# One transformer layer on one core: pairs of column tiles, the top-k search and its masks, and the copies of the normed input rearranged

## The chip, the cores and the metric

The kernel runs on one core of a Trainium2 chip. The metric is the device time of one execution in microseconds (us). A change of over 0.2% (5 us here) is about what a measurement of this kernel can tell from no change.

The core's engines work side by side and wait for each other through semaphores: TensorE (PE, matrix products, results in the accumulator memory PSUM), VectorE (DVE), ScalarE (ACT), GpSimd (POOL) and SyncE (SP, which here only starts DMA transfers). Each engine takes its own instructions strictly in the order in which the program lists them.

## The reference, cut to what matters

```python
h = rmsnorm(x, pre_norm_mix) * (1 + scale_m) + shift_m          # (1024, 1024)
proj = h @ w_in                                                # q_lat, kv_lat, k_idx, w_idx, z, xbc, dt, g_a, g_b
# A: sparse attention: a score for every pair of positions, the best 256 keys of each query
iscore = sum_h w_idx * relu(q_idx[h] @ k_idx.T)                # -inf for later chunks
idx = top_k(iscore, 256)
y_a = softmax(q @ kv[idx] * scale + bias) @ kv[idx] @ w_uv @ w_o_attn
# B: Mamba-2 mixer: causal convolution of width 4 over xbc, SiLU, chunked scan, gate silu(z)
y_b = ssd(silu(conv(xbc)), z, dt) @ w_o_ssd
x = x + gate_m * rmsnorm((sigmoid(g_a)*y_a + sigmoid(g_b)*y_b) @ w_out)
x = x + gate_f * rmsnorm((silu(h2 @ wg) * (h2 @ wu)) @ w_ffn_out)
```

All of it is in float32. A float32 product is made of three products of split operands: each operand is kept as a rounded part (`hi`) and a rest (`lo`), and hi·hi, hi·lo and lo·hi are added up in PSUM. So every weight tile passes through ACT (`hi`, a copy that rounds) and POOL (`lo`, raw minus hi) before PE can use it.

## The kernel before, in words

The input h is held as eight tiles of 128 features by 1024 positions, each in two halves of 512 positions (`Hs[k][hi or lo][half]`). The stages that matter here follow one another in the program, and a scheduler, which has a model of the engines, interleaves them. The program's order is its priority.

1. **The input** (`k_h`, L364). x is normed and scaled into h. Each half tile of h in full precision is also written to DRAM (`d_h`), from ACT's queue (L375, L438).
2. **First projections, convolution tiles, indexer.** PE multiplies h by columns of `w_in`. `conv` (L776) is one convolved tile: 48 products of 128x512 in two PSUM banks, one ACT copy for each, nine DVE operations that add the shifted taps (L783 to L785), then SiLU. `convs(FIRST)` (L896) makes five groups of four tiles. Beside them the indexer (L599 to L637) adds 16 heads into the scores `acc[i]`, one SBUF tile for each block i = 2 to 7 of 128 queries, (i+1)·128 keys wide.
3. **Sums for pairs** (L640 to L658). Copies of h come back from `d_h` and are combined on DVE into the operands of a seven-product scheme (Winograd's form of Strassen's) for two column tiles and two halves of positions; `d_h12` saves those parts of h whose places are used up.
4. **Pairs of column tiles** (`h_early`, `h_pair`, L847 to L899). For the twelve pairs that make z and the gate g_a, two products of 12 matmuls each were made early (`h_early`); `h_pair` makes the other five. It loads four weight halves (a11, a12, a21, a22), adds them up (`hs` s1 on DVE, L864; s2 and others on POOL, L865, L879, L883), turns each into hi and lo (L820 ACT, L821 POOL), and DVE reads the products out of PSUM in five additions (L873 twice, L881, L885, L893). Three PSUM banks serve these products. a22's place (tag `vt`, L856) exists once.
5. **The search** (`Ranked`, L663 to L733). The 256 best keys of a query are found by a search for the 256th score, bit by bit, for all six blocks at once: 33 steps. In a step, a candidate value for each block (`cand`, one column of 128 values for each) is compared with all scores. ACT counts for blocks 7, 5 and 2 (L692), DVE for 6, 4 and 3 (L680, an operation that also sums what it writes, followed by a read of the sum). Then four DVE operations on 128x6 values decide and make the next candidate: `tm` = count <= bound (L685), `tm` = tm·cand (L686), `c` = max(c, tm) (L687), `cand` from `c` and `ce` (L727, in the first eight steps L721). All of these small tiles are in SBUF.
6. **The masks** (`mark`, L735). Six passes over each block's scores turn the found value into a mask of 0 and -1e30 (`MK[i]`), ties taken in order (L738 to L747). They are made for all blocks together, straight after the search.
7. **Attention** (L1035), eight head pairs of four query groups each, in the order u = 0, 2, 1, 3. u = 0 needs no mask; u = 2 needs blocks 4 and 5. The first operation that adds a mask or bias to scores is L962. The last three convolution groups (`convs(LATER)`, L1080) and further products fill PE beside it.

The weight stream `W` has three hi and three lo places and loads two tiles ahead of the one in use.

Of the kernel before, what the change touches and what calls it, by code (L numbers as in the profile page):

```python
# [67 lines left out]
def build(tc, a, dbg=None, stop=99, slots=None):  # L68
# [290 lines left out]
        ada_end(k, acc)  # L359
        first[k] = split(Q, raw, "p1", (P, 3, P), lo_eng=G)  # L360

    raws = []

    def k_h(k, b):  # L364
        x = X0[k][b]
        V.tensor_tensor(x, x, rx[b], op=OP.mult)
        hi, lo = H_(f"h{k}h", dt=F32R), H_(f"h{k}l", dt=F32R)
        i1 = S.activation(hi, x, AF.Identity, bias=mod[:, k:k + 1], scale=amul[:, k:k + 1])
        V.tensor_scalar(x, x, amul[:, k:k + 1], mod[:, k:k + 1], op0=OP.mult, op1=OP.add)
        i2 = (G if b else V).tensor_tensor(lo, x, f(hi), op=OP.subtract)  # L370
        if k == 5:
            barrier.update((i.ins.engine, i.ins.name) for i in (i1, i2))
        Hs[k][0][b], Hs[k][1][b] = hi, lo
        for t, dst in raws:
            S.dma_start(dst, t)  # L375
        raws[:] = [(x, d_h[k][:, half(b)])]
        dump("h", x, (k, slice(None), half(b)))

    def k_mm(k, b):
# [17 lines left out]
    with in_order(*ORDERED):  # L397
        sums = [None, None], [None, None]
        x_squares(0, range(8), sums[0])
        r0 = rstd(sums[0], D)  # L400
        k_ada(0)
        pr0 = rspread(r0)
        k_mod(0)
        rx[0] = Q("rx")
        S.activation(rx[0], pr0, AF.Copy)
        pp1 = [[(bank if t or b else bank_d)(f"pp{t}") for b in BS] for t in range(3)]
        k_h(0, 0)
        k_ada(1)
# [12 lines left out]
        k_mod(2)  # L421
        k_h(0, 1)
        k_h(1, 1)
        k_mm(0, 1)
        k_mm(1, 1)
        for k in range(AHEAD, KT):
            k_h(k, 0)
            k_h(k, 1)
            if k < KT - 1:
                i = k_load(k + 1).ins  # L430
                barrier[i.engine] = i.name
                k_ada(k + 1)
            k_mm(k, 0)
            if k < KT - 1:
                k_mod(k + 1)
            k_mm(k, 1)
        for t, dst in raws:
            S.dma_start(dst, t)  # L438
        const_loads()
        nA = con.tile([P, 32], F32, name="nA")  # L440
        S.activation(nA, alb, AF.Exp)
# [197 lines left out]

    XH = {n: [None] * 4 for n in ("11", "21", "22", "1", "2", "3", "4")}  # L640
    for j in range(4):
        for i in range(2):
            SP.dma_start(d_h12[j, i], f(Hs[j][i][1]))
    for j in range(4):
        top, low = R("htop"), R("hlow")
        SP.dma_start(top, d_h[j])
        SP.dma_start(low, d_h[4 + j])
        b11, b12, b21, b22 = (t[:, half(b)] for t in (top, low) for b in BS)
        for n, k, b in (("11", j, 0), ("21", 4 + j, 0), ("22", 4 + j, 1)):
            XH[n][j] = Hs[k][0][b], Hs[k][1][b]  # L650
        V.tensor_tensor(b11, b12, b11, op=OP.subtract)
        XH["1"][j] = split(Q, b11, "ht", lo_eng=G)
        V.tensor_tensor(b12, b22, b12, op=OP.subtract)
# [9 lines left out]
    class Ranked:  # L663
# [3 lines left out]
        def __init__(self, on_s, on_v):  # L667
            self.tiles, self.ns = on_s + on_v, len(on_s)
            self.n = [(i + 1) * P for i in self.tiles]
            for name in ("c", "ce", "cand", "cnt", "kk", "ks", "kv", "sg", "tm"):  # L670
                setattr(self, name, sm.tile([P, len(self.tiles)], F32, name=name + "_", tag="rk" + name, bufs=1))
            self.junk = [Q("junk", (P, 1024), BF) for _ in range(2)]

        def rows(self):
# [6 lines left out]

        def take(self, sl, bound):

            c, cand, tm = self.c[:, sl], self.cand[:, sl], self.tm[:, sl]
            V.tensor_tensor(tm, self.cnt[:, sl], bound[:, sl], op=OP.is_le)  # L685
            V.tensor_tensor(tm, tm, cand, op=OP.mult)  # L686
            V.tensor_tensor(c, c, tm, op=OP.max)  # L687
# [29 lines left out]
        def bits(self):  # L717
# [9 lines left out]
                V.scalar_tensor_tensor(cand, self.ce, 2.0 ** -e, c, op0=OP.mult, op1=OP.add)  # L727
                self.step()
            sl = slice(0, self.ns)
            V.scalar_tensor_tensor(cand[:, sl], c[:, sl], 1.5 * 2.0 ** -24, c[:, sl], op0=OP.mult, op1=OP.add)  # L730
            V.tensor_scalar(cand[:, sl], cand[:, sl], TINY, None, op0=OP.max)
            self.count_v(OP.is_lt, cand, self.rows()[sl])
            self.take(sl, self.kv)  # L733

        def mark(self):  # L735

            for x, y in self.rows():
                V.tensor_scalar(y, y, self.c[:, x:x + 1], self.sg[:, x:x + 1], op0=OP.subtract, op1=OP.mult)  # L738
            self.count_v(OP.is_gt, 0.0, self.rows())
            V.tensor_scalar(self.tm, self.cnt, -1.0, float(TOPK), op0=OP.mult, op1=OP.add)  # L740
            for x, d in self.rows():
                eq, run = R("eq")[:, 0:self.n[x]], R("run")[:, 0:self.n[x]]
                V.tensor_scalar(eq, d, 0.0, None, op0=OP.is_equal)
                V.tensor_tensor_scan(run, eq, eq, 0.0, op0=OP.add, op1=OP.max)
                V.scalar_tensor_tensor(run, run, self.tm[:, x:x + 1], eq, op0=OP.is_le, op1=OP.mult)
# [9 lines left out]
    best = Ranked((7, 5, 2), (6, 4, 3))  # L755
    best.start()
    best.bits()
    best.mark()
    if dbg is not None and "mk" in dbg:
        for i in MK:  # L760
            n = (i + 1) * P
# [28 lines left out]
            S.activation(t, t, AF.Silu)  # L790
            SP.dma_start(dst, t)

    def conv_group(g, n):

        tiles = ((16 + g, d_bc[g, 0]), (24 + g, d_bc[g, 1]), (2 * g, d_xs[2 * g]), (2 * g + 1, d_xs[2 * g + 1]))
        for i in range(0, 4, n):
            outs = [o for t in tiles[i:i + n] for o in conv(*t)]
            if n > 1:
                with in_order(mybir.EngineType.Activation):
                    conv_out(outs[::-1])  # L800
# [2 lines left out]

    n_x = iter(range(GROUPS))

    def convs(kinds):
        for kind in kinds:
            conv_group(next(n_x), 2 if kind == "X" else 1)


    PAIRS = [((1 + t, d_z[t]), (2 + t, d_z[t + 1]), AF.Silu) for t in range(0, 16, 2)]
# [40 lines left out]
    def h_pair(n):  # L852
        (ca, da), (cb, db), fn = PAIRS[n]
        a11, a12 = (hw(W.tile(0, F32), ca, h) for h in range(2))
        a21 = hw(wp.tile([P, 4, P], F32, name="a21", tag="adaw", bufs=2), cb, 0)
        a22 = hw(vp.tile([P, 4, P], F32, name="a22", tag="vt", bufs=1), cb, 1)  # L856
        if n < H_EARLY:
            p, p1 = bank_d("ph"), EV("p1")
            SP.dma_start(p1, d_q1[n])
# [797 lines left out]
```

## Time and profile before

| | |
|---|---|
| median of 3 runs | 2538.54 us (2537.05 to 2541.62) |
| the profiled execution | 2529.57 us |
| its span, first to last instruction | 2527.3 us |
| PE busy in the span | 2388.9 us (95%), 11802 matmuls |
| DVE, ACT, POOL busy | 1591.7 (63%), 1211.8 (48%), 1139.5 us (45%) |
| DMA | 372.72 MB, mean 147 GB/s |

A profile row of a group gives the program line, the engine, the operation, output<-inputs by the program's tile names, shapes and count; behind the bar the busy time in us and the mean of one in ns; behind the second bar the engine's idle time before them and what ended it. A row of the timeline gives the start, the duration, and in brackets the idle time before it. Rows by stretch of time give the busy time of each engine with its number of instructions, then the TensorE clock that was granted (1.00 is full), the share of the DMA engines and GB/s.

### The profile page before, as it was taken

How to read it: one execution, taken by the hardware profiler on the slowest of the kernel's cores; microseconds unless marked ns; L12 is line 12 of the kernel's file. 1: busy time of each engine (PE TensorE's matmuls, PEld its weight loads, DVE VectorE, ACT ScalarE, POOL GpSimd, SP SyncE). 2: the span in 40 equal slices, each digit the busy share in tenths (PEclk: the TensorE clock that was granted, in tenths of full speed). 3: DMA queues.
4: the chain of work that ended last, by engine and by line, in shares of the span. 5: the costliest groups of instructions: out<-in, count | busy, mean ns of one | idle time of the engine just before them, and what ended most of it. 6: DMA issues, size and time to landing. Idle time of an engine off the chain costs nothing. (4 is left out here: it accounts for less than half of the span.)

```text
span 2527.3 us, 35118 instructions
## 1 busy us (share of the span) xinstructions
PE 2388.9 (95%) x11802; PEld 1919.3 (76%) x11802; DVE 1591.7 (63%) x2984; ACT 1211.8 (48%) x2331; POOL 1139.5 (45%) x909
## 2 busy tenths in 40 slices
PE   6999999988868999999999999999999999999996
PEld 5788888766557887777776776888777888888886
DVE  3465767899997556767557767346476666543336
ACT  3445666566624454555666556454445222343111
POOL 2432213645554344555234444656667554532233
PEclk8999999989989999999999999999999999999998
DMA  8234242533353222222578676565375444344132
GB/s 311 104 105 143 81 137 101 196 113 108 117 171 103 85 99 92 89 88 79 179 221 259 217 236 220 186 212 192 125 246 167 163 156 152 117 150 147 46 101 88
DMA packets 228675, 372.72 MB, mean 147 GB/s; under 512 B 23008, under 2 KB 87184, under 8 KB 228496
## 3 DMA queue, kind: packets, MB, share of 16 engines
q1 hardware_dynamic: 225472, 365.72, 43.9%
q10 hardware_dynamic: 3024, 4.77, 0.5%
q8 instruction: 93, 1.52, 0.3%
q14 instruction: 86, 0.70, 0.1%
HBM read 273.65 MB, written 99.90 MB: 148 GB/s over the span
## 5 line engine op out<-in xcount | busy, mean ns | idle before, releaser
L152 POOL TENSOR_TENSOR wlo<-wraw,whi 128x512 fp32r<-128x512 f32 (+1 forms) x234 | 319.7, 1367 | 564.2 <-ACT whi L151 493.5
L151 ACT ACTIVATE whi<-wraw 128x512 fp32r<-128x512 f32 (+1 forms) x234 | 145.5, 623 | 319.4 <-PE pfo L231 111.4
L1419 PE MATMUL p<-xh,wr 128*128 128x512 f32 x880 | 274.2, 391 | 2.7 <-DVE g L1469 2.7
L1413 POOL TENSOR_TENSOR wr<-a,wr 128x512 fp32r<-128x512 f32 x110 | 154.4, 1417 | 101.8 <-ACT wr L1412 68.4
L1419 PEld LDWEIGHTS p<-xh,wr 128*128 128x128 f32 x880 | 166.0, 189 | 37.7 <-DVE g L1469 3.2
L1419 PE MATMUL p<-xl,wr 128*128 128x512 f32 x440 | 171.9, 391 | 0.0
L965 ACT ACTIVATE lg<-lg,mx 128x256 f32<-128x256 f32 (+7 forms) x128 | 98.3, 769 | 96.2 <-DVE mx L962 93.4
L322 POOL TENSOR_TENSOR adaw<-adaw,cs 128x512 f32<-128x512 f32 x64 | 69.6, 1087 | 128.5 <-DMA adaw<-ada_w 119.6
L1412 ACT ACTIVATE wr<-a 128x512 fp32r<-128x512 f32 x110 | 67.7, 628 | 122.8 <-PE p L1419 95.7
L231 PE MATMUL pfo<-ah,wlo 128*128 128x512 f32 x304 | 118.1, 389 | 0.0
L231 PE MATMUL pfo<-al,whi 128*128 128x512 f32 x304 | 117.9, 389 | 0.0
L231 PE MATMUL pfo<-ah,whi 128*128 128x512 f32 x304 | 117.8, 389 | 0.0
L637 DVE SCALAR_TENSOR_TENSOR acc<-rel,widx,acc 128x384 f32<-128x384 f32 (+2 forms) x90 | 92.1, 1046 | 37.5 <-ACT rel L632 37.3
L1534 DVE TENSOR_TENSOR facc<-facc,pfo 128x512 f32<-128x512 f32 x64 | 44.0, 687 | 112.0 <-PE pfo L231 112.0
L1419 PE MATMUL p<-h2h,wr 128*128 128x512 f32 x352 | 112.3, 396 | 0.0
L692 ACT ACTIVATE junk<-acc,cand__2341 128x1024 bf16<-128x1024 f32 (+2 forms) x96 | 86.2, 898 | 54.3 <-DVE cand__2341 L727 38.0
L828 PE MATMUL ph<-hth,whi 128*128 128x512 f32 x192 | 83.5, 435 | 23.2 <-DVE g L873 12.0
L231 PE MATMUL pos<-yw,whi 128*128 128x512 f32 x256 | 101.3, 396 | 3.8 <-DVE yw L1262 3.6
L231 PE MATMUL pos<-yh,whi 128*128 128x512 f32 x256 | 100.6, 393 | 1.7 <-ACT yh L1261 1.7
L231 PE MATMUL pos<-yh,wlo 128*128 128x512 f32 x256 | 99.9, 391 | 0.0
L828 PE MATMUL ph<-hth,wlo 128*128 128x512 f32 x192 | 81.7, 436 | 18.2 <-POOL wlo L821 18.1
L1419 PEld LDWEIGHTS p<-xl,wr 128*128 128x128 f32 x440 | 82.9, 188 | 17.3
(642 smaller groups left out, 7220.6 us busy)
## 6 DMA issues: line engine op xcount, KB each, us to landing
wraw<-w_in SPq DMA_DIRECT2D x130, 256.0 KB, 2.7
a<-w_ffn_in SPq DMA_DIRECT2D x124, 256.0 KB, 3.1
adaw<-ada_w SPq DMA_DIRECT2D x64, 256.0 KB, 2.6
al<-d_ac SPq DMA_DIRECT2D x32, 512.0 KB, 5.5
wraw<-w_o_ssd SPq DMA_DIRECT2D x64, 256.0 KB, 3.2
al<-d_a SPq DMA_DIRECT2D x44, 256.0 KB, 5.1
d_a<-g SPq DMA_DIRECT2D x40, 256.0 KB, 2.5
ada<-ada_p SPq DMA_DIRECT2D x16, 512.0 KB, 5.9
```

The lines of the kernel that those rows point to most:

```text
L151: behind(S.activation(hi[:, :kt], raw[:, :kt], AF.Copy))
L152: behind(G.tensor_tensor(lo[:, :kt], raw[:, :kt], f(hi[:, :kt]), op=OP.subtract))
L231: T.matmul(o, wt[:, k0 + i, :], xs[k][xi][b][:, sl], start=pi == 0 and i == 0 and wt is hi and xi == 0, stop=pi == len(pcs) - 1 and i == l ...
L322: behind(G.tensor_tensor(t, t, cs[:, 4 * h:4 * h + 4, None].to_broadcast([P, 4, P]), op=OP.mult))
L637: V.scalar_tensor_tensor(acc[i][:, 0:n], rel[:, 0:n], ws, acc[i][:, 0:n], op0=OP.mult, op1=OP.add)
L692: S.activation(self.junk[0][:, 0:self.n[x]], y, AF.Sign, scale=-1.0, bias=self.cand[:, x:x + 1], accum_out=self.cnt[:, x:x + 1])
L828: T.matmul(p, w[wi][:, i], XH[x][i][xi], start=start and i == 0 and k == 0, stop=i == 3 and k == 2, skip_group_check=True)
L965: S.activation(lg[:, 0:n], lg[:, 0:n], AF.Exp, scale=-1.0, bias=m, accum_out=mx[:, 3:4])
L1412: S.activation(w[:, 0], src, AF.Copy)
L1413: G.tensor_tensor(w[:, 1], src, f(w[:, 0]), op=OP.subtract)
L1419: T.matmul(p, w[:, wi, i], X[x][i][xi], start=start and i == 0 and k == 0, stop=i == 3 and k == 2, skip_group_check=True)
L1534: V.tensor_tensor(fv, fv, p[b], op=OP.add)
```

## The change

Five edits, with the line numbers of the kernel before:

- `h_pair`: a22 lies in `vt` for odd pairs and in another existing place (`ul`, which the weights of the indexer and of attention use) for even ones.
- `Ranked`: `c`, `ks`, `kv` and `tm` become columns of one PSUM bank, taken from the five that other stages share. `tm·cand` gets a place of its own in SBUF, `got`. So each of a step's four small operations has an input in PSUM and at most one in SBUF. Two copies are added at the search's end: c to `got`, and c to `found` in SBUF, from which the masks are made.
- `mark` makes one block's mask. It is called in the order 4, 5, 2, 3, 6, 7, and it stands behind the pairs in the program, with the first of the three later convolution groups: two calls inside that group, four behind it. The other two groups stay where they were.
- The writes of h to `d_h` from ACT's queue go. In their place, behind the start of the indexer, POOL adds hi and lo of each half into a tile `hraw` (one place, 128x1024) and SP writes it, eight times.
- The writes to `d_h12` move behind those.

```diff
 def k_h(k, b):
...
-        for t, dst in raws:
-            S.dma_start(dst, t)
-        raws[:] = [(x, d_h[k][:, half(b)])]
...
+    with tc.issue_after(next(i for i in reversed(nc.cur_bb.bb.instructions) if i.engine == mybir.EngineType.Pool)):
+        for k in range(KT):
+            t = vp.tile([P, L], F32, name="hraw", tag="vt", bufs=1)
+            for b in BS:
+                G.tensor_tensor(t[:, half(b)], f(Hs[k][0][b]), f(Hs[k][1][b]), op=OP.add)
+            ins = SP.dma_start(d_h[k], t).ins
+    with tc.issue_after(ins):
+        for j in range(4):
+            for i in range(2):
+                SP.dma_start(d_h12[j, i], f(Hs[j][i][1]))
...
-            for name in ("c", "ce", "cand", "cnt", "kk", "ks", "kv", "sg", "tm"):
+            for name in ("found", "cand", "cnt", "kk", "sg", "ce", "got"):
                 setattr(self, name, sm.tile([P, len(self.tiles)], F32, name=name + "_", tag="rk" + name, bufs=1))
+            rk = bank("rank")
+            for i, name in enumerate(("c", "ks", "kv", "tm")):
+                setattr(self, name, rk[:, 8 * i:8 * i + len(self.tiles)])
...
             V.tensor_tensor(tm, self.cnt[:, sl], bound[:, sl], op=OP.is_le)
-            V.tensor_tensor(tm, tm, cand, op=OP.mult)
-            V.tensor_tensor(c, c, tm, op=OP.max)
+            V.tensor_tensor(got, tm, self.cand[:, sl], op=OP.mult)
+            V.tensor_tensor(c, c, got, op=OP.max)
...
-        def mark(self):
+        def mark(self, i):
...
-    best.mark()
...
-        a22 = hw(vp.tile([P, 4, P], F32, name="a22", tag="vt", bufs=1), cb, 1)
+        a22 = hw((vp if n % 2 else wp).tile([P, 4, P], F32, name="a22", tag="vt" if n % 2 else "ul", bufs=1), cb, 1)
...
+    marks = iter((4, 5, 2, 3, 6, 7))
+    convs(LATER[0], lambda: best.mark(next(marks)))
+    for i in marks:
+        best.mark(i)
...
-    convs(LATER)
+    convs(LATER[1:])
```

What the scheduler makes of it, at three places. The first is DVE in the middle of the search, beside a pair in the middle of the twelve. `g` and `u` are products read out of PSUM, `junk,cnt` are counts, the rest the small operations. Before:

```order
L685 TENSOR_TENSOR tm__2347<-cnt__2342,ks__2344 128x6
L686 TENSOR_TENSOR tm__2347<-tm__2347,cand__2341 128x6
L687 TENSOR_TENSOR c__2339<-c__2339,tm__2347 128x6
L873 TENSOR_TENSOR g_5698<-ph,p_5676 128x512
L727 SCALAR_TENSOR_TENSOR cand__2341<-ce__2340,c__2339 128x6
L680 TENSOR_SCALAR junk,cnt__2342<-acc_997,cand__2341 128x896
L680 TENSOR_SCALAR junk,cnt__2342<-acc_995,cand__2341 128x640
L873 TENSOR_TENSOR u_5699<-ph,p_5676 128x512
L680 TENSOR_SCALAR junk,cnt__2342<-acc_999,cand__2341 128x512
```

The same place in the changed kernel, whose lines are numbered a little higher and where `rank` is the PSUM bank:

```order
L689 TENSOR_TENSOR rank<-cnt__2357,rank 128x6
L878 TENSOR_TENSOR g_5879<-ph,p_5857 128x512
L690 TENSOR_TENSOR got__2361<-rank,cand__2356 128x6
L691 TENSOR_TENSOR rank<-rank,got__2361 128x6
L731 SCALAR_TENSOR_TENSOR cand__2356<-ce__2360,rank 128x6
L684 TENSOR_SCALAR junk,cnt__2357<-acc_981,cand__2356 128x896
L684 TENSOR_SCALAR junk,cnt__2357<-acc_979,cand__2356 128x640
L878 TENSOR_TENSOR u_5880<-ph,p_5857 128x512
L684 TENSOR_SCALAR junk,cnt__2357<-acc_1023,cand__2356 128x512
```

The kinds of operation are the same; each small one now names `rank`. Counted over DVE's whole list, 33 steps stand ahead of the last product of the twelfth pair (L893) before, and 27 in the changed kernel: six steps moved behind the pairs.

The second place is DVE straight behind the search's 32nd step before (the last pair's products are still to come; `acc` rows are the first pass of the masks):

```order
L730 SCALAR_TENSOR_TENSOR cand__2341<-c__2339 128x3
L738 TENSOR_SCALAR acc_997<-acc_997,c__2339,sg__2346 128x896
L738 TENSOR_SCALAR acc_995<-acc_995,c__2339,sg__2346 128x640
L738 TENSOR_SCALAR acc_999<-acc_999,c__2339,sg__2346 128x512
L731 TENSOR_SCALAR cand__2341<-cand__2341 128x3
L873 TENSOR_TENSOR g_6133<-ph,p_6111 128x512
```

and in the changed kernel a step behind the last pair, with the taps of a convolved tile (`cv`) between:

```order
L684 TENSOR_SCALAR junk,cnt__2357<-acc_981,cand__2356 128x896
L787 SCALAR_TENSOR_TENSOR cv<-pw,vec,cv 128x511
L684 TENSOR_SCALAR junk,cnt__2357<-acc_979,cand__2356 128x640
L324 TENSOR_REDUCE adas<-adaw 128x128
L684 TENSOR_SCALAR junk,cnt__2357<-acc_1023,cand__2356 128x512
L788 SCALAR_TENSOR_TENSOR cv<-pw,vec,cv 128x1
L789 SCALAR_TENSOR_TENSOR cv<-pw,vec,cv 128x511
L787 SCALAR_TENSOR_TENSOR cv<-pw,vec,cv 128x510
L689 TENSOR_TENSOR rank<-cnt__2357,rank 128x6
```

The end of the search and the masks now lie among convolved tiles. Counted up to the first L962, DVE has six sets of tap rows (L783) behind the pairs before and fifteen now; PE has 113 convolution matmuls (`pw`) between the last pair product and the first score product of attention before, and 249 now.

The third place is POOL at the start of the indexer (`wlo` are the lo parts of weight tiles, `r` a small power). Before:

```order
L152 TENSOR_TENSOR wlo<-wraw,whi 128x512 x2
L270 TENSOR_TENSOR r<-v,nhalf 128x4
L152 TENSOR_TENSOR wlo<-wraw,whi 128x512 x11
L270 TENSOR_TENSOR r<-v,nhalf 128x4
L152 TENSOR_TENSOR wlo<-wraw,whi 128x512
```

and now:

```order
L270 TENSOR_TENSOR r<-v,nhalf 128x4
L567 TENSOR_TENSOR hraw<-h0h,h0l 128x512 x2
L152 TENSOR_TENSOR wlo<-wraw,whi 128x512 x2
L567 TENSOR_TENSOR hraw<-h1h,h1l 128x512 x2
L567 TENSOR_TENSOR hraw<-h2h,h2l 128x512 x2
L152 TENSOR_TENSOR wlo<-wraw,whi 128x512
L567 TENSOR_TENSOR hraw<-h3h,h3l 128x512 x2
L152 TENSOR_TENSOR wlo<-wraw,whi 128x512
L567 TENSOR_TENSOR hraw<-h4h,h4l 128x512 x2
L152 TENSOR_TENSOR wlo<-wraw,whi 128x512
```

Sixteen additions now stand among the weight parts, two for each tile of h. On SP's queue the eight writes of `hraw` stand one by one between loads of weights (L150), and the eight writes to `d_h12`, which were among the first loads of the program, stand behind the last of them.

More of the change, by code (lines that the diff above doesn't have):

```diff
@@ L360, in k_mod @@
         first[k] = split(Q, raw, "p1", (P, 3, P), lo_eng=G)
-    raws = []
     def k_h(k, b):
@@ L436, in build @@
             k_mm(k, 1)
-        for t, dst in raws:
-            S.dma_start(dst, t)
         const_loads()
@@ L641, in build @@
     for j in range(4):
-        for i in range(2):
-            SP.dma_start(d_h12[j, i], f(Hs[j][i][1]))
-    for j in range(4):
         top, low = R("htop"), R("hlow")
@@ L682, in take @@
         def take(self, sl, bound):
-            c, cand, tm = self.c[:, sl], self.cand[:, sl], self.tm[:, sl]
+            c, tm, got = self.c[:, sl], self.tm[:, sl], self.got[:, sl]
             V.tensor_tensor(tm, self.cnt[:, sl], bound[:, sl], op=OP.is_le)
-            V.tensor_tensor(tm, tm, cand, op=OP.mult)
-            V.tensor_tensor(c, c, tm, op=OP.max)
+            V.tensor_tensor(got, tm, self.cand[:, sl], op=OP.mult)
+            V.tensor_tensor(c, c, got, op=OP.max)
         def step(self):
@@ L729, in bits @@
             sl = slice(0, self.ns)
-            V.scalar_tensor_tensor(cand[:, sl], c[:, sl], 1.5 * 2.0 ** -24, c[:, sl], op0=OP.mult, op1=OP.add)
+            V.tensor_copy(self.got[:, sl], c[:, sl])
+            V.scalar_tensor_tensor(cand[:, sl], self.got[:, sl], 1.5 * 2.0 ** -24, c[:, sl], op0=OP.mult, op1=OP.add)
             V.tensor_scalar(cand[:, sl], cand[:, sl], TINY, None, op0=OP.max)
@@ L733, in bits @@
             self.take(sl, self.kv)
-        def mark(self):
[L737 to L741, printed above, removed]
+            V.tensor_copy(self.found, c)
+        def mark(self, i):
+            for x, d in [self.rows()[self.tiles.index(i)]]:
+                V.tensor_scalar(d, d, self.found[:, x:x + 1], self.sg[:, x:x + 1], op0=OP.subtract, op1=OP.mult)
+                self.count_v(OP.is_gt, 0.0, [(x, d)])
+                V.tensor_scalar(self.kk[:, x:x + 1], self.cnt[:, x:x + 1], -1.0, float(TOPK), op0=OP.mult, op1=OP.add)
                 eq, run = R("eq")[:, 0:self.n[x]], R("run")[:, 0:self.n[x]]
@@ L744, in mark @@
                 V.tensor_tensor_scan(run, eq, eq, 0.0, op0=OP.add, op1=OP.max)
-                V.scalar_tensor_tensor(run, run, self.tm[:, x:x + 1], eq, op0=OP.is_le, op1=OP.mult)
+                V.scalar_tensor_tensor(run, run, self.kk[:, x:x + 1], eq, op0=OP.is_le, op1=OP.mult)
                 V.scalar_tensor_tensor(run, d, 0.0, run, op0=OP.is_gt, op1=OP.max)
@@ L791, in conv_out, with conv_group @@
             SP.dma_start(dst, t)
-    def conv_group(g, n):
+    def conv_group(g, n, beside):
         tiles = ((16 + g, d_bc[g, 0]), (24 + g, d_bc[g, 1]), (2 * g, d_xs[2 * g]), (2 * g + 1, d_xs[2 * g + 1]))
@@ L797, in conv_group @@
             outs = [o for t in tiles[i:i + n] for o in conv(*t)]
+            beside()
             if n > 1:
@@ L804, in build, with convs @@
     n_x = iter(range(GROUPS))
-    def convs(kinds):
+    def convs(kinds, beside=lambda: None):
         for kind in kinds:
-            conv_group(next(n_x), 2 if kind == "X" else 1)
+            conv_group(next(n_x), 2 if kind == "X" else 1, beside)
     PAIRS = [((1 + t, d_z[t]), (2 + t, d_z[t + 1]), AF.Silu) for t in range(0, 16, 2)]
```

## The prediction

> **What bounds the kernel now.** I first read the busy time by stretches of time, cut at the stages of the program.
>
> ```profile
> 318.00:442.00 124.00, 124.00 (x578) 104.04 (x577) 80.81 (x113) 81.30 (x159) 28.58 (x20) 1.00 0.37 119
> 442.00:518.00 76.00, 67.94 (x279) 52.89 (x279) 62.94 (x98) 41.20 (x76) 48.90 (x33) 0.96 0.55 181
> 518.00:708.00 190.00, 156.56 (x605) 116.69 (x603) 177.23 (x368) 127.82 (x253) 102.11 (x82) 0.95 0.33 113
> 708.00:782.00 74.00, 51.64 (x213) 41.80 (x214) 71.84 (x100) 12.35 (x21) 39.97 (x27) 0.84 0.49 164
> 782.00:960.00 178.00, 178.00 (x1024) 146.73 (x1023) 105.39 (x331) 94.10 (x178) 69.41 (x66) 1.00 0.28 94
> ```
>
> The first pair of numbers behind the stretch is PE's busy time and count, then weight loads, DVE, ACT, POOL. Ahead of 442 us and behind 782 us PE is busy without a gap. Between 518 us (the first pair's last sum) and 782 us (attention's first L962) it isn't, and there DVE is busy for 177.23 + 71.84 = 249.1 of 264 us, 94%. The pairs, the search and the masks run in this stretch: DVE bounds it, PE the stages on both sides.
>
> How much PE loses follows from the pace of matmuls that wait for nothing: the first and the last of twelve in a row.
>
> ```profile
> 722.73 0.39 PE L828 MATMUL ph<-h4h,whi 128*128 128x512 f32 x1
> ...
> 725.22 0.39 PE L828 MATMUL ph<-h7h,wlo 128*128 128x512 f32 x1
> ```
>
> They start (725.22 - 722.73) / 11 = 0.226 us apart. The 605 of the second stretch need 137 us and take 190. So a pair of 60 matmuls needs 13.6 us and takes 18.8.
>
> PE's waits in 518 to 782 us, with total, number and longest, and the longest one's row:
>
> ```profile
> PE ph L828 <- POOL wlo L821: 17.7, 10, 1.8
> PE pw L231 <- DVE cv L784: 17.1, 2, 14.8
> PE ph L828 <- DVE g L873: 12.0, 7, 3.2
> ...
> 760.90 1.19 PE L231 MATMUL pw<-h,whi 128*128 128x512 f32 x2 [14.77 <-DVE cv L784]
> ```
>
> Two of the three end on DVE; the long one falls among the masks, where PE has run ahead into the later convolutions, its three PSUM banks are full, and DVE's taps stand behind mask passes. The first wait is a chain that begins on DVE: `hs`, POOL, ACT, POOL.
>
> What fills DVE, as groups from 440 to 825 us (mean ns is the number ahead of the second bar):
>
> ```profile
> L680 DVE TENSOR_SCALAR_CACHE_REDUCE junk<-acc,cand__2341 128x896 bf16<-128x896 f32 (+4 forms) x99 | 91.3, 922 | 2.2
> L727 DVE SCALAR_TENSOR_TENSOR cand__2341<-ce__2340,c__2339 128x6 f32<-128x6 f32 x23 | 17.1, 744 | 0.6
> L687 DVE TENSOR_TENSOR c__2339<-c__2339,tm__2347 128x6 f32<-128x6 f32 (+1 forms) x33 | 15.6, 473 | 0.8
> L686 DVE TENSOR_TENSOR tm__2347<-tm__2347,cand__2341 128x6 f32<-128x6 f32 (+1 forms) x33 | 14.9, 451 | 1.1 <-DVE tm__2347 L685 0.2
> L685 DVE TENSOR_TENSOR tm__2347<-cnt__2342,ks__2344 128x6 f32<-128x6 f32 x32 | 10.3, 322 | 5.3 <-ACT junk L692 3.7 <-DVE junk L680 0.5
> L783 DVE SCALAR_TENSOR_TENSOR cv<-pw,vec,cv 128x511 f32<-128x511 f32 (+2 forms) x13 | 9.6, 736 | 1.5 <-ACT cv L780 1.5
> L873 DVE TENSOR_TENSOR u<-ph,p 128x512 f32<-128x512 f32 x12 | 8.2, 685 | 0.0
> L653 DVE TENSOR_TENSOR htop<-hlow,htop 128x512 f32<-128x512 f32 x4 | 4.9, 1235 | 2.5 <-DMA hlow<-d_h 2.5
> L721 DVE TENSOR_SCALAR cand__2341<-c__2339 128x6 f32<-128x6 f32 x8 | 4.7, 582 | 0.2
> L784 DVE SCALAR_TENSOR_TENSOR cv<-pw,vec,cv 128x1 f32<-128x1 f32 (+2 forms) x12 | 2.5, 209 | 1.6 <-ACT cv L780 1.6
> ```
>
> 129 operations on six columns (L727, L687, L686, L685, L721) take 62.6 us. The timeline says why. DVE at the end of two steps, and POOL beside it:
>
> ```profile
> 706.22 1.21 DVE L686 TENSOR_TENSOR tm__2347<-tm__2347,cand__2341 128x6 f32<-128x6 f32 x1
> ...
> 707.95 0.70 DVE L687 TENSOR_TENSOR c__2339<-c__2339,tm__2347 128x6 f32<-128x6 f32 x1
> 708.69 1.20 DVE L727 SCALAR_TENSOR_TENSOR cand__2341<-ce__2340,c__2339 128x6 f32<-128x6 f32 x1
> ...
> 713.25 0.17 DVE L686 TENSOR_TENSOR tm__2347<-tm__2347,cand__2341 128x6 f32<-128x6 f32 x1
> 713.46 0.17 DVE L687 TENSOR_TENSOR c__2339<-c__2339,tm__2347 128x6 f32<-128x6 f32 x1
> ```
>
> ```profile
> 706.12 1.28 POOL L883 TENSOR_TENSOR wraw<-wraw,hs 128x512 f32<-128x512 f32 x1
> 707.37 2.50 POOL L821 TENSOR_TENSOR wlo<-hs,whi 128x512 fp32r<-128x512 f32 x2
> ```
>
> The same operation takes 1.21 us while POOL works and 0.17 us while it doesn't, and the slow ones end with POOL's: 707.43 against 707.40, 709.89 against 709.87. They are locked out by POOL. L873, whose inputs are one in PSUM and one in SBUF, is not: 0.685 us on average, in the same company, while L653, of the same size with both inputs in SBUF, takes 1.235.
>
> **The change part by part.** Times are the profiled execution's: a span of 2527.3 us in 2529.6. The median of the runs is 2538.5, 9 us above it; I carry the difference over.
>
> *Small operations in PSUM.* Each has now one SBUF input at most, like L873. Their price without POOL: the trace has no 128x6 operation on PSUM; the nearest is L784 (a PSUM input, one column) at 0.209, and dependent ones add about 0.04 (0.21 between the starts of L686 and L687 at 0.17 each). I take 0.25: 129 x 0.25 = 32 us instead of 62.6, 30 us saved. Bounds: 0.17, the clean SBUF row, saves 41; 0.40, near L686's mean today, saves 11. [...]
>
> *Masks and steps beside convolutions.* DVE does six of its 33 steps and all masks behind the pairs, among 15 sets of taps instead of 6. Up to the first L962 that adds 9 L783, 8 L785 of the same length and 8 L784: 17 x 0.736 + 8 x 0.209 = 14 us. The masks' passes are the same; the two copies cost 0.4.
> DVE's work in the stretch is then 249 - 30 + 14 = 233 us. What share of the time will it be busy? In a pair it has five sums and `hs` (6 x 0.685 = 4.1), and 27/11 = 2.45 steps of three counts (3 x 0.922) and four small ones (1.0): 9.2. That is 13.3 us against PE's 13.6: equal, so neither hides the other's delays as DVE does today at 94%. I take 91%: 233 / 0.91 = 256, and L962 starts at 518 + 256 = 774, 8 us earlier. At 94% it is 17 us, at 88% it is 1 us later. What is late next is PE itself in the pairs and still DVE behind them.
> By then PE has done 249 - 113 = 136 more matmuls of the later convolutions: 136 x 0.226 = 31 us that the stage behind, which PE bounds (178 of 178 us), no longer has to do. Together 39 us.
>
> *a22's second place.* It lets the loads of the next pair run earlier, against the 17.7 us of waits for `wlo`. As DVE bounds the stretch I count nothing; the cover is DVE's 13.3 us in a pair. If DVE had more room it would be worth up to those 17.7.
>
> *Less to fill attention with.* Without filler attention runs like this:
>
> ```profile
> 1000.00:1200.00 200.00, 194.69 (x1389) 151.62 (x1388) 140.84 (x540) 106.68 (x246) 116.60 (x119) 1.00 0.26 85
> ```
>
> 97%, against 100% with it: up to 5 us over the 178; I take 2 lost.
>
> *Copies of h.* The writes from ACT's queue fell in part into the first 63 us, where the DMA engines carry 311 GB/s:
>
> ```profile
> GB/s 311 104 105 143 81 137 101 196 113 108 117 171 103 85 99 92 89 88 79 179 221 259 217 236 220 186 212 192 125 246 167 163 156 152 117 150 147 46 101 88
> d_h<-x ACTq DMA_DIRECT2D x16, 256.0 KB, 2.2
> ```
>
> If half of the 16 and of the eight `d_h12` writes fall there, 3.1 MB go: at most 10 us; I take 2, since other waits remain. The additions cost POOL 16 x 1.3 us where it is mostly idle, but each of the eight rounds holds POOL until SP's 512 KB write lands, with weight parts behind it, and SP's loads of weights behind the write. Their pace and the price of a landing:
>
> ```profile
> 172.40 1.29 POOL L152 TENSOR_TENSOR wlo<-wraw,whi 128x512 fp32r<-128x512 f32 x1 [8.53 <-ACT whi L151]
> 175.12 1.30 POOL L152 TENSOR_TENSOR wlo<-wraw,whi 128x512 fp32r<-128x512 f32 x1 [1.43 <-ACT whi L151]
> 184.48 1.29 POOL L152 TENSOR_TENSOR wlo<-wraw,whi 128x512 fp32r<-128x512 f32 x1 [8.06 <-ACT whi L151]
> ...
> vt<-d_v SPq DMA_DIRECT2D x8, 512.0 KB, 3.6
> ada<-ada_p SPq DMA_DIRECT2D x16, 512.0 KB, 5.9
> ```
>
> Two parts are wanted every 12.1 us, one every 6.0. A round takes 2.6 + 3.6 to 2.6 + 5.9 = 6.2 to 8.5 us and lets one part through. Seven rounds fall 1 to 18 us behind; loading two tiles ahead covers 12.1. So 0 to 5 us; I take 2 lost.
>
> Sum: 39 - 2 + 2 - 2 = 37 us. 2529.6 - 37 = 2492.6 for a profiled execution, 2538.5 - 37 = 2501 for the median. With one bound at a time it is 2489 (0.17 us), 2522 (0.40 us), 2493 (94%) and 2510 (88%); 0.17 us with all 10 us of the writes gives 2481. So this case reaches from 2481 to 2522.
>
> **The rivals.**
> *The copies bound the first stage (slower).* A round's write stands on SP behind writes that wait for ACT, or lands late, and PE, which has no gap there, waits for `wlo`. A round of c us costs 7 x (c - 6.0) - 12.1. It eats the 39 us and 5 more from c = 14.0; at 15 it costs 51 and the time is 2550. For it: the single place of `hraw` and the strict queues. Against: 256 KB writes land in 2.2 us. Chance 0.07.
> *The lock stays.* If an output in SBUF is enough to be locked out, the small operations keep their 62.6 us: 249 + 14 = 263, at 94% 279 us, L962 15 us later, 31 - 15 - 2 = 14 us gained: 2524. Against it stands L873, which writes to SBUF. Chance 0.12. [...]
> *The credit is lost.* If attention needs that filler, only the 8 us are left: 2530. Against: the 97%. Chance 0.08.
> *Both engines full.* At 0.17 and 94%, 222 us of work take 236: 28 + 31 us, less nothing else: 2479. Chance 0.12.
> *It comes to nothing.* Small losses of each kind add up to the gain, within 5 us of 2538.5. Chance 0.06.
>
> **How the numbers follow.** The forecast has 0.55. 0.2% (5 us) is about what a measurement tells from no change. Faster: 0.55 + 0.12 + 0.12 + 0.07 of the lost credit = 0.86; the same 0.07; slower 0.07. The range from 2474 to 2531 holds most of the forecast, of the full engines, of the staying lock and half of the lost credit, about 0.8.
>
> **What would show it.** In the changed profile the small operations' means should lie near 0.25 us whatever POOL does; a mean over 0.4 is the staying lock. The first L962 should start near 774 us, and a pair should take about 15 us of PE instead of 18.8. The 14.77 us wait should be gone. Ahead of 442 us PE should stay without gaps; gaps behind `wlo` near 160 to 220 us are the slower rival. If the stretch to L962 isn't shorter and the stage behind it not shorter by some 30 us, the argument is wrong.

## The result, and the profile after

The changed kernel takes 2471.34 us (median of 4, 2468.4 to 2477.29), the kernel before on the same chip 2537.8 us: a ratio of 0.9743, with an interval of 0.9717 to 0.9769. The forecast was 2501 us with a range from 2474 to 2531, so the direction was right and the gain, 66 us, was nearly double the 37 forecast. Between the two profiled executions the spans differ by 60.7 us; the profile accounts below add up to that.

The busy time by stretches of the changed kernel, cut where the prediction cut the old one: two stretches ahead of the first pair's last sum (513.1 us), the eleven further pairs up to the twelfth's last sum (660.7 us), the time behind them up to the first addition of a mask or bias (749.0 us; it was 782.2), and the attention behind. The prediction had 774 us for this addition. The columns are those of the prediction's first fence.

```profile
311.00:436.00 125.00, 125.00 (x582) 104.87 (x582) 81.14 (x114) 81.83 (x159) 28.06 (x20) 1.00 0.38 119
436.00:513.10 77.10, 69.06 (x298) 53.90 (x297) 65.50 (x87) 42.18 (x78) 54.01 (x35) 1.00 0.56 187
513.10:660.70 147.60, 146.77 (x647) 120.97 (x646) 130.79 (x351) 119.05 (x235) 109.39 (x87) 1.00 0.54 174
660.70:749.00 88.30, 69.23 (x297) 55.92 (x296) 83.50 (x163) 33.21 (x60) 36.27 (x28) 0.92 0.39 128
749.00:926.00 177.00, 169.52 (x1016) 138.50 (x1016) 106.55 (x363) 94.11 (x186) 69.45 (x68) 0.98 0.27 85
```

For comparison, the same two stretches of the kernel before, pairs and behind them:

```profile
518.20:735.40 217.20, 179.90 (x693) 135.43 (x693) 202.61 (x406) 134.22 (x265) 116.63 (x92) 0.94 0.39 134
735.40:782.20 46.80, 28.29 (x126) 23.06 (x126) 46.66 (x61) 5.79 (x9) 25.24 (x17) 0.82 0.29 96
```

The eleven pairs took 217.2 us and take 147.6. At the 0.226 us of a matmul that waits for nothing, 693 matmuls need 156.6 us, so PE lost 60.6 us there; 647 need 146.2, so it loses 1.4. PE is now the bound in the pairs: 13.4 us each. Behind the pairs it lost 46.8 - 126 x 0.226 = 18.3 us and loses 88.3 - 297 x 0.226 = 21.2. I use this count, length less matmuls times 0.226, for every run below. PE's busy time alone would show less of the loss, though it too grows where PE waits: 179.90 us for 693 matmuls is 0.260 each, 146.77 for 647 is 0.227. Part of that growth is a lower granted clock, 0.94 in the pairs of the kernel before and 1.00 in the changed one. Behind this wait of the kernel before, matmuls start 0.43 us apart and not 0.23, and the clock granted from 708.68 to 711.83 us is 0.51:

```profile
708.68 0.79 PE L828 MATMUL ph<-hth,wlo 128*128 128x512 f32 x1 [1.79 <-POOL wlo L821]
709.27 0.63 PE L828 MATMUL ph<-hth,whi 128*128 128x512 f32 x1
709.70 0.63 PE L828 MATMUL ph<-htl,whi 128*128 128x512 f32 x1
710.12 0.63 PE L828 MATMUL ph<-hth,wlo 128*128 128x512 f32 x1
```

So lost time, as counted here, is waits and slower matmuls together.

What PE waits for between 513 and 749 us in the changed kernel (total, number, longest):

```profile
PE pw L231 <- DVE cv L788: 16.4, 3, 8.1
PE pw L231 <- POOL wlo L152: 1.2, 1, 1.2
PE ph L833 <- DVE kk__2358 L711: 0.8, 1, 0.8
```

The waits of the pairs, for `wlo` (17.7 us) and for DVE's `g` (12.0), are gone. What is left are three waits for taps, all behind the pairs, where DVE is busy for 83.5 of 88.3 us; the longest is 8.1 us, where the kernel before had 14.8. The small operations of the search, DVE's groups of the changed kernel (in the line numbers of the changed kernel, L689 to L691, L731 and L725 are the old L685 to L687, L727 and L721):

```profile
L691 DVE TENSOR_TENSOR rank<-rank,got__2361 128x6 f32<-128x6 f32 (+1 forms) x33 | 5.6, 170 | 0.8
L689 DVE TENSOR_TENSOR rank<-cnt__2357,rank 128x6 f32<-128x6 f32 (+1 forms) x33 | 5.6, 169 | 7.0 <-ACT junk L696 5.8 <-DVE junk L684 0.5
...
L690 DVE TENSOR_TENSOR got__2361<-rank,cand__2356 128x6 f32<-128x6 f32 (+1 forms) x33 | 5.4, 162 | 0.8
...
L731 DVE SCALAR_TENSOR_TENSOR cand__2356<-ce__2360,rank 128x6 f32<-128x6 f32 x23 | 3.7, 160 | 0.7
...
L725 DVE TENSOR_SCALAR cand__2356<-rank 128x6 f32<-128x6 f32 x8 | 1.3, 161 | 0.2
```

They took 62.6 us together and take 21.6, at 0.16 to 0.17 us each.

### The profile page after: what moved, and what is told of

Read it like the earlier page. It is cut to its first block, busy times and chain, and to the rows that moved or that the text cites. A ratio compares the mean times of both kernels' runs of the same rounds, so it can differ in the third digit from the quotient of the medians.

```text
span 2466.6 us, 35119 instructions
## 1 busy us (share of the span) xinstructions
PE 2362.2 (96%) x11802; PEld 1912.0 (78%) x11802; DVE 1551.4 (63%) x2991; ACT 1209.9 (49%) x2329; POOL 1155.5 (47%) x925
## 5 line engine op out<-in xcount | busy, mean ns | idle before, releaser
L636 ACT ACTIVATE rel<-prel 128x512 f32<-128x512 f32 (+3 forms) x160 | 77.6, 523 | 34.7 <-PE prel L635 31.2
L1422 POOL TENSOR_TENSOR wr<-s,wr 128x512 fp32r<-128x512 f32 x44 | 61.9, 1416 | 69.1 <-ACT wr L1421 65.5
```

The lines of the kernel that those rows point to most:

```text
L636: S.activation(rel[:, 512 * b:512 * b + w_], pr[:, 0:w_], AF.Relu)
L1422: G.tensor_tensor(w[:, 1], src, f(w[:, 0]), op=OP.subtract)
```

## The experiments

Eleven runs followed. Four undo one part of the change, one is the changed kernel again, three have a single part on the kernel before, one has two parts together, and two go on from what was found. All ratios are to runs of the kernel before on the same chip, which took 2528 to 2538 us (median) on the four chips. "Pairs" and "behind" are PE's lost time in those two stretches, by the count above.

| kernel | ratio (interval) | median us | pairs | behind |
|---|---|---|---|---|
| before | 1 | 2537.8 | 60.6 | 18.3 |
| changed | 0.9743 (0.9717 to 0.9769) | 2471.3 | 1.4 | 21.2 |
| changed, again | 0.9765 (0.9748 to 0.9782) | 2469.1 | 1 | 22 |
| changed, operands in SBUF | 0.9927 (0.9906 to 0.9947) | 2514.4 | 35.9 | 22.5 |
| changed, one place for a22 | 0.9890 (0.9870 to 0.9910) | 2504.3 | 32.5 | 22.0 |
| changed, masks as before | 0.9772 (0.9752 to 0.9792) | 2472.6 | 1.0 | 28.1 |
| changed, copies as before | 0.9784 (0.9767 to 0.9800) | 2476.4 | 1.0 | 20.4 |
| before + operands in PSUM | 0.9883 (0.9868 to 0.9899) | 2499.9 | 29.2 | 21.0 |
| before + second place | 0.9954 (0.9937 to 0.9971) | 2517.0 | 37.0 | 31.0 |
| before + both | 0.9793 (0.9765 to 0.9821) | 2482.2 | 1.0 | 30.3 |
| before + masks beside convolutions | 1.0006 (0.9993 to 1.0020) | 2533.8 | 59.5 | 19.1 |
| changed + two mask passes on ACT | 0.9733 (0.9717 to 0.9750) | 2460.6 | 1.0 | 13.8 |
| the same + PSUM banks | 0.9692 (0.9660 to 0.9725) | 2454.5 | 0.9 | 7.9 |

**The small operands back in SBUF.**

```diff
-            rk = bank("rank")
+            rk = sm.tile([P, 32], F32, name="rank", tag="rank", bufs=1)
```

> The changed kernel with the search's four small operands back in SBUF, everything else as changed. Theory A (DVE bounds the stretch from the first pair to the first L971, and the lock by POOL was what filled it): the 129 small operations go from about 0.17 us back to about 0.48 us, 129 x 0.31 = 40 us, and nearly all of it shows: 2471 + 40 = 2511 us, first L971 some 40 us later, pairs slower than 13.4 us. Theory B (a22's second place freed the pairs, PE bounds them and hides the small operations): half of the steps are hidden in pairs that stay at 13.4 us of PE, 10 to 15 us later, 2484 us.

Measured 0.9927 against 0.9743 and 0.9765 of the changed kernel: 41 to 47 us. Theory A's size. The groups of the same five operations in this kernel:

```profile
L691 DVE TENSOR_TENSOR rank<-rank,got__2361 128x6 f32<-128x6 f32 (+1 forms) x33 | 21.8, 661 | 0.9
L690 DVE TENSOR_TENSOR got__2361<-rank,cand__2356 128x6 f32<-128x6 f32 (+1 forms) x33 | 20.8, 629 | 0.9
...
L689 DVE TENSOR_TENSOR rank<-cnt__2357,rank 128x6 f32<-128x6 f32 (+1 forms) x33 | 12.6, 383 | 3.6 <-ACT junk L696 2.9
...
L731 DVE SCALAR_TENSOR_TENSOR cand__2356<-ce__2360,rank 128x6 f32<-128x6 f32 x23 | 9.4, 409 | 0.7
...
L725 DVE TENSOR_SCALAR cand__2356<-rank 128x6 f32<-128x6 f32 x8 | 6.6, 827 | 0.3
...
L708 DVE TENSOR_SCALAR sg__2359<-rank 128x6 f32<-128x6 f32 x1 | 1.2, 1221 | 0.0
```

That is 71.2 us instead of 21.6: the lock costs 49.6 us of DVE in this kernel. It falls on L725 and L708 too, which read one SBUF tensor and no second one: 827 ns on average and 1221 ns here, 161 and 166 in the changed kernel, where that tensor is in PSUM. The kernel before has the same on L721, the old L725: it took 0.17 us from 551.46 us, while POOL did nothing, and 1.22 us from 540.41 us, where it ended at 541.63 us and POOL's subtraction at 541.60.

**One place for a22.**

```diff
-        a22 = hw((vp if n % 2 else wp).tile([P, 4, P], F32, name="a22", tag="vt" if n % 2 else "ul", bufs=1), cb, 1)
+        a22 = hw(vp.tile([P, 4, P], F32, name="a22", tag="vt", bufs=1), cb, 1)
```

> The changed kernel with a22 of every pair in the one old place, everything else as changed. Theory A: DVE's work is the same, the chain of loads was only late because DVE was late; at most 5 us later, 2471 to 2476 us. Theory B: the loads of a pair's a22 wait for the pair before, the waits for wlo (17.7 us before the change) come back, a pair takes 15 us of PE or more: 15 to 20 us later, 2486 to 2491 us.

Measured 0.9890: 32 to 37 us, double what even theory B asked. Theory A is wrong on this part. The stretch of pairs in this kernel:

```profile
509.80:696.90 187.10, 165.91 (x684) 131.06 (x683) 157.78 (x421) 133.93 (x267) 115.14 (x92) 0.96 0.45 154
```

DVE is busy for 84% and PE still loses 32.5 us. Neither of them bounds the pairs then; a chain of waits does.

**Masks and convolutions as before.** After the search all masks are made in one go, and all three groups of convolutions stand behind the first attention:

```diff
     best.bits()
+    for i in best.tiles:
+        best.mark(i)
...
-    marks = iter((4, 5, 2, 3, 6, 7))
-    convs(LATER[0], lambda: best.mark(next(marks)))
-    for i in marks:
-        best.mark(i)
...
-    convs(LATER[1:])
+    convs(LATER)
```

> The changed kernel with all six masks in one go behind the search and all three late convolution groups behind the first attention in the program's order, as before the change; the rest as changed. Theory A (the convolutions that PE can do beside the masks are a credit for the stage behind): the stretch loses the 14 us of extra taps but the stage behind gets 27 us longer, and the long wait for cv comes back: 13 to 27 us later, 2484 to 2498 us. Theory B (PE had enough to do anyway): within 5 us of 2471.

Measured 0.9772, 2 to 7 us above the changed kernel, by which of its two ratios is taken: nearer to theory B. Behind the pairs PE loses 28.1 us instead of 21.2.

**Copies as before.**

```diff
-    with tc.issue_after(next(i for i in reversed(nc.cur_bb.bb.instructions) if i.engine == mybir.EngineType.Pool)):
-        for k in range(KT):
-            t = vp.tile([P, L], F32, name="hraw", tag="vt", bufs=1)
...
+        for t, dst in raws:
+            S.dma_start(dst, t)
+        raws[:] = [(x, d_h[k][:, half(b)])]
```

> The changed kernel with the copies of h as before the change: written from ACT's queue in the start stage, and the eight writes of d_h12 where they stood; no additions on GpSimd. Theory A (the start's writes took DMA time from the weights that PE waits for, 5.8 us, and the additions cost 1 to 2 us later): 4 to 6 us later, 2475 to 2477 us. Theory B (the start gained from something else, the additions cost nothing): within 2 us of 2471.

Measured 0.9784, 5 to 10 us above the changed kernel. The place is the start. From 40 to 60 us of this kernel, and of the changed one:

```profile
40.00:60.00 20.00, 18.09 (x98) 12.95 (x88) 8.48 (x18) 7.21 (x12) 7.29 (x6) 0.74 0.75 254
```

```profile
40.00:60.00 20.00, 20.00 (x120) 14.22 (x118) 10.75 (x21) 7.54 (x13) 8.30 (x6) 0.93 0.39 137
```

With the writes gone the DMA engines' share falls from 0.75 to 0.39 there, and PE makes 120 matmuls instead of 98 (113 in the changed kernel's second run). The price of the additions, from 160 to 200 us, of this kernel and of the changed one:

```profile
160.00:200.00 40.00, 39.09 (x185) 31.90 (x184) 26.36 (x54) 22.65 (x35) 8.20 (x7) 1.00 0.25 87
```

```profile
160.00:200.00 40.00, 38.12 (x175) 30.29 (x174) 30.80 (x54) 22.12 (x34) 23.69 (x18) 1.00 0.52 187
```

POOL works 15.5 us more, DVE's 54 instructions take 4.4 us longer, and PE makes 10 matmuls fewer: at most 2.3 us here (the two kernels stand at places 6 us apart in the program).

**The changed kernel again.** It was run a second time, unaltered, beside the next kernels.

> The changed kernel itself once more, so that the others of this call have it on the same chip: 0.974 of the kernel before.

Measured 0.9765; the two ratios, 0.9743 and 0.9765, are the mark for everything undone above.

**The small operands in PSUM alone, on the kernel before.** The first experiment showed what the lock costs with everything else in place, this one what its removal gives without the rest. The edit is that of `Ranked` in the change.

> The kernel before with the search's small operands in PSUM alone. In the pairs PE lost 60 us before the change (217 us less 693 matmuls of 0.226 us), 1 us after it, 36 with the operands back in SBUF and 33 with the single place of a22. Theory C (two causes whose delays add, the lock on DVE and the late a22): the pairs lose about 33 us here, 27 less than before, 2538 - 27 = 2511 us, 0.989 of before. Theory D (each cause alone is enough to hold PE, so that taking one away lets the other in): within 10 us of before, 0.996 or more.

Measured 0.9883, 29 us: theory C. What PE waits for here, from 510 to 800 us:

```profile
PE pw L231 <- DVE cv L790: 19.9, 2, 15.4
PE ph L835 <- POOL wlo L828: 18.1, 11, 1.8
```

The 17.7 us of waits for `wlo` have not moved, though DVE has 41 us less to do. They are a22's. How, the timeline of this kernel shows at one pair's end, first POOL, then SP's queue, DVE and PE:

```profile
584.39 1.29 POOL L828 TENSOR_TENSOR wlo<-a,whi 128x512 fp32r<-128x512 f32 x1 [1.42 <-ACT whi L827]
589.15 1.29 POOL L872 TENSOR_TENSOR hs<-hs,wraw 128x512 f32<-128x512 f32 x1 [3.46 <-DVE hs L871]
590.40 1.30 POOL L886 TENSOR_TENSOR a<-wraw,a 128x512 f32<-128x512 f32 x1
591.65 1.29 POOL L890 TENSOR_TENSOR wraw<-wraw,hs 128x512 f32<-128x512 f32 x1
592.90 2.51 POOL L828 TENSOR_TENSOR wlo<-hs,whi 128x512 fp32r<-128x512 f32 x2
```

```profile
585.71 0.33 SPq L822 DMA_DIRECT2D a<-w_in  x1
```

```profile
588.38 0.69 DVE L871 TENSOR_TENSOR hs<-a,a 128x512 f32<-128x512 f32 x1 [0.31 <-issue]
```

```profile
594.22 0.50 PE L835 MATMUL ph<-hth,wlo 128*128 128x512 f32 x1 [1.76 <-POOL wlo L828]
```

POOL's last reading of a22 ends at 585.68 us; the load of the next pair's a22 into the same place goes out at 585.71 (in the kernel before such loads land 2.7 us after their issue, by the median); the sum that needs it starts 2.7 us later; then come POOL's subtraction, two more that stand ahead in its order, and `wlo`. PE has the first `wlo` 8.5 us after the place came free, and one pair later all of it comes again (589.15 to 604.65 us on POOL: 15.5 us a pair).

**a22's second place alone, on the kernel before.** The edit is the reverse of the diff above.

> The kernel before with a22's second place alone. Theory C: the pairs lose about 36 us, 24 less than before, 2538 - 24 = 2514 us, 0.990 of before, and the waits for wlo (17.7 us) are gone while the small operations keep 0.4 to 0.7 us. Theory D: within 10 us of before, 0.996 or more. My prediction's own step (worth nothing while DVE bounds): the same as before.

Measured 0.9954, 12 us. In the pairs theory C is right: 37.0 us lost, 23.6 less than before. What PE waits for from 510 to 800 us:

```profile
PE pw L231 <- DVE cv L784: 25.6, 4, 11.1
PE ph L828 <- ACT junk L692: 7.6, 3, 2.8
PE ph L828 <- DVE g L873: 7.2, 2, 4.3
...
PE ph L828 <- POOL wlo L821: 0.4, 1, 0.4
```

The waits for `wlo` fell to 0.4 us; those for DVE, and for ACT behind the search's counts, stay. But behind the pairs 31.0 us are lost instead of 18.3. The order of the program has changed too: 28 of the search's 33 steps now stand ahead of the last pair's last sum, where the kernel before has all of them there. The decision of the 33rd step (L685) starts at 742.8 us, 38 us behind that sum, where in the kernel before it started 12 us ahead of it. I had left this out, so the whole came to half of the 24 us expected.

**The two together, on the kernel before.**

> The kernel before with the small operands in PSUM and a22's second place together, masks and copies as before the change. Theory C (the pairs lose 60.8 us to two causes that add): the pairs lose 1 to 3 us here, as in the changed kernel, and the masks, behind which less PE work lies, lose about 28 us as in the run with the masks undone, 10 more than before the change; 59 - 10 = 49 us less than before, 0.980 to 0.982. If the two parts needed the masks or the copies to work, the pairs would lose 10 us or more and it would stay above 0.985.

Measured 0.9793: 52 us, as expected. The pairs lose 1.0 us with neither masks nor copies changed, so these two parts are the whole of the pairs' gain.

**The masks beside convolutions alone.** The edits of `mark`, `conv_group` and `LATER` alone, operands in SBUF.

> The kernel before with the masks one by one beside the convolutions, alone (operands in SBUF, one place for a22, the old copies). Theory: where the pairs are slow the steps of the search are nearly done behind them and PE loses 18.5 us there; the masks beside the convolutions can save part of that, 0 to 7 us: 0.997 to 1.000. My prediction's step (31 us of convolutions done earlier are a credit): 0.988 to 0.991.

Measured 1.0006, with an interval that leaves no gain of more than 0.07%. The credit of 31 us that the prediction put here does not come by this part: PE makes 818 matmuls in the two stretches together, 819 before.

**Two mask passes on ACT.** What is lost now lies behind the pairs, on DVE, while ACT is busy for 33.2 of 88.3 us.

```diff
-                V.tensor_scalar(d, d, self.found[:, x:x + 1], self.sg[:, x:x + 1], op0=OP.subtract, op1=OP.mult)
+                S.activation(d, d, AF.Identity, bias=self.found[:, x:x + 1], scale=self.sg[:, x:x + 1])
...
-                V.tensor_scalar(MK[self.tiles[x]], run, 1.0, -NEG, op0=OP.subtract, op1=OP.mult)
+                S.activation(MK[self.tiles[x]], run, AF.Identity, bias=self.ce[:, 0:1], scale=-NEG)
```

(`found` then holds -found·sg, and `ce` holds -1e30.)

> The changed kernel with two of the eight passes of each mask on ScalarE in place of VectorE (the difference to the found value, 5.7 us for six tiles, and the last pass that writes the mask, 3.3 us). Theory: behind the pairs DVE is the bound (83.5 of 88.3 us busy) and PE loses 20 us there, waiting for taps that stand behind masks; 9 us less on DVE are 6 to 9 us less in all, 2462 to 2465 us where the changed kernel takes 2471. Rival (the wait there is set by ACT's and SP's turn for the convolutions, or the passes on ACT stand behind others and DVE waits for them): within 3 us of the changed kernel, or slower.

Measured 0.9733 against 0.9765 of the changed kernel on the same chip: 2460.6 against 2469.1 us, 8.5 less. The stretch behind the pairs:

```profile
659.90:740.80 80.90, 67.48 (x297) 54.63 (x296) 75.79 (x153) 41.60 (x70) 36.14 (x28) 0.94 0.41 140
```

The same 297 matmuls in 80.9 us instead of 88.3, with 7.7 us less on DVE: DVE bounds this stretch.

**More PSUM banks for the convolutions beside the masks.**

```diff
-        p = [bank_d("pw") for b in BS]
+        p = [bank_d("pw"), (more or bank_d)("pw")]
...
-    convs(LATER[0], lambda: best.mark(next(marks)))
+    convs(LATER[0], lambda: best.mark(next(marks)), bank)
```

> The changed kernel with the two mask passes on ScalarE as in the run above, and the second PSUM bank of each convolved tile beside the masks taken from the five banks of the other pool, so that PE can run about three tiles ahead of the taps and not one and a half. Theory: the 12.4 us that PE still waits for taps there go down to a few, 8 to 12 us less than with the passes alone (2460.6 at 0.9733): about 0.969. Rival: attention's scores, which want these banks, come later, and the gain there is given back: 0.972 or more.

Measured 0.9692 (0.9660 to 0.9725), the fastest of all. PE's lost time behind the pairs falls from 13.8 to 7.9 us, less than I expected, and the waits for taps stay at 9.6 us against 12.4. That the time fell below the kernel without the banks is likely and not settled: the two ran on different chips, and the upper end of the interval, 0.9725, lies 0.0008 under 0.9733, whose own interval reaches down to 0.9717.

## Why the prediction was wrong in size

**What bounds the stretch.** Wrong by half, and this is the step that failed. The prediction took one bound, DVE at 94%, and costed every other part by whether DVE has room. The pairs had two holds. Each alone still costs PE 29 to 37 of the 60.6 us, and only without both is PE the bound. That a stretch shows an engine at 94% did not say that nothing else holds PE.

Over the whole stretch, from the first pair's last sum to the first addition of a mask or bias, the two parts do different things. The numbers are the sums of the two stages:

| kernel | small operands | places for a22 | length, us | DVE busy, us | matmuls |
|---|---|---|---|---|---|
| before | SBUF | 1 | 264.0 | 249.3 | 819 |
| before + masks beside convolutions | SBUF | 1 | 263.5 | 248.7 | 818 |
| before + second place | SBUF | 2 | 272.1 | 260.8 | 903 |
| changed, operands in SBUF | SBUF | 2 | 271.3 | 262.3 | 942 |
| before + operands in PSUM | PSUM | 1 | 235.3 | 209.4 | 819 |
| changed, one place for a22 | PSUM | 1 | 239.4 | 210.1 | 818 |
| before + both | PSUM | 2 | 236.3 | 211.4 | 907 |
| changed, masks as before | PSUM | 2 | 231.8 | 210.8 | 897 |
| changed | PSUM | 2 | 235.9 | 214.3 | 944 |

The small operands go with the stretch's length, as the prediction said of DVE's work: 263 to 272 us with them in SBUF, 232 to 239 in PSUM. a22's second place goes with the matmuls that PE makes meanwhile: 818 or 819 with one place, 897 to 944 with two.

**a22's second place, "I count nothing".** The failed step as it stood in the sum; what the place brings was booked under the masks instead (below). It is worth 32 to 37 us with the lock gone and 12 without. The "up to 17.7" named beside it was too low as well, because the waits for `wlo` are only the end of that chain that PE shows. The rows to read were POOL's waits in the kernel before, 518 to 736 us, which the prediction does not use:

```profile
POOL wlo L821 <- ACT whi L820: 49.0, 19, 4.4
POOL hs L865 <- DVE hs L864: 35.2, 10, 3.6
```

Ten pairs of eleven show 3.5 us in which POOL waits for one DVE sum. This looked like DVE being late, and I called it "a chain that begins on DVE". The same row has 36.9 us with the operands in PSUM alone and 5.8 in the changed kernel:

```profile
POOL hs L872 <- DVE hs L871: 36.9, 10, 4.2
```

```profile
POOL hs L870 <- DVE hs L869: 5.8, 6, 1.2
```

So it began at the load. One thing is not separated: the scheduler plans the order of all engines with the places that it has, so a second place also changes that order. In every kernel with one place all 33 steps stand ahead of the last pair's last sum, in every kernel with two places 27 or 28. How much of a22's worth is the earlier load and how much the other order stays open.

**The price of a small operation in PSUM, 0.25 us.** Mis-sized: 0.16 to 0.17. Instead of 30 us, 41 went from DVE's busy time (62.6 less 21.6), which was the bound of 0.17 us that the prediction named. L689 to L691 read PSUM and take no longer, 0.162 to 0.170 us on average, than an operation of the same shape on SBUF in the kernel before that POOL didn't hold, 0.172 us (it started at 508.99 us, and POOL had ended its last operation at 508.01):

```profile
L704 DVE TENSOR_SCALAR sg__2346<-tm__2347 128x6 f32<-128x6 f32 x1 | 0.2, 172 | 0.0
```

The rival "the lock stays" fell: with one input in PSUM, an output in SBUF was not locked. L690 took 162 ns on average, and 0.15 us from 540.71 us, in the middle of a subtraction of POOL's (540.00 to 541.32 us).

**Masks and steps beside convolutions: 8 us earlier and 31 us of credit.** The first half was mis-sized, the second put down to the wrong edit. The sum of 39 us meant that PE's lost time in the stretch would fall from 79 to 40 us; it fell to 22.6. The stretch is 28 us shorter, not 8. The 91% of DVE came out as assumed ((130.8 + 83.5) / 235.9), but with 214 us of work where I had 233. Of these 19 us, 11 are the price of a small operation, above, and 6.5 the passes of the masks, which I had taken as unchanged: 47.6 us before, 41.1 in the changed kernel. It seems that POOL held some of these before as well, for a pass over 512 columns, most of it beside a subtraction of POOL's (767.08 to 769.22 us), took 1.509 us, longer than the 0.681 of the same pass over 1024; no run tests it:

```profile
L743 DVE TENSOR_SCALAR eq<-acc 128x512 f32<-128x512 f32 x1 | 1.5, 1509 | 0.0
...
L743 DVE TENSOR_SCALAR eq<-acc 128x1024 f32<-128x1024 f32 x1 | 0.7, 681 | 0.0
```

The credit came nearly at its size, 944 - 819 = 125 matmuls or 28 us, but with a22's second place, which I had counted at nothing. Between the last pair product and the first score product, PE has 113 convolution matmuls in the kernel before and 118 with the masks' part alone, but 234 with a22's second place alone and 249 in the changed kernel. That the size fitted was luck. The masks' part gives nothing alone (1.0006), and undone it costs 2 to 7 us. What it does do is to pay back, from 28 to 21 us, some of what faster pairs push behind them.

**Less to fill attention with, 2 us.** Right in kind. From the first addition on, the kernel before takes 1745.1 us for 8723 matmuls, the changed one 1717.6 for 8580: 27.5 us less for 143 x 0.226 = 32, so 5 us lost.

**The copies, +2 and -2.** The writes were under-costed: the last product by the root-mean-square of x (L366) starts at 79.7 us, not 85.5 (81.2 in the changed kernel's second run). The rounds of additions cost PE up to 2.3 us at the place where they were expected to, and the slower rival, 51 us lost behind them, did not come. Together 5 to 10 us of gain where I had zero. So the profile's 60.7 us are 56 us in the stretch and 9 ahead of it (the first pair's sum comes 5.1 us earlier, with 18 more matmuls done), less 5 in attention.

**The range.** Its lower end, 2474, came from full engines with a22 at zero. Two bounds that were named were never put together: 0.17 us a small operation (2489) and 17.7 us for a22's place. Together they give the measured 2471, but by luck, as the terms under them were wrong. Of the rivals, "both engines full" (2479) came nearest; in the pairs PE did become full, with DVE busy for 89%.

## What to carry to other kernels

Before an edit is costed at nothing because another engine is the bound, follow one repeated wait to its end, on the engine that waits in the middle of the chain and not only on the one that counts: here 3.5 us before the same instruction in nearly every round went back to a load that couldn't start. Two holds in one stage can add up: of the 60.6 us that PE lost in the pairs, taking one away gave back 31.4 or 23.6, and taking away both gave back 59.6. What a part is worth in the whole depends on the rest: 32 to 47 us undone from the changed kernel, 12 to 29 added to the old one. Count a stage's gain as time that the bounding engine loses, its length less matmuls times their pace. Then a shorter stage (28.1 us here) and work done earlier in it (28.2 us) are the two halves of one sum, and each may come from a different edit.

## What was not expected of the hardware

The same 11802 matmuls keep PE busy for 2388.9 us in the kernel before and 2362.2 in the changed one: behind some waits the granted clock is about half (0.51 in the rows above) and matmuls start 0.43 us apart, behind others it is 1.00 (634.44 to 638.00 us, behind a wait of 1.78 us for `wlo`). What decides between them no run here tests. The price of the lock depends on the company: the same operation of the search takes 0.473 us on average (L687) in the kernel before, 0.661 (L691) in the changed kernel with operands in SBUF, where the pairs are faster and POOL is busy for 59% of them and not 54%, and 0.170 in PSUM.
